# Retention in seven quarter products: keys paired with queries, values with gates

## The chip, the cores and the metric

The kernel runs on one core of a Trainium2 chip. The metric is the device time of one execution in microseconds (us); the time of a kernel is the median of its runs. The engines are named as in the profile: PE (TensorE, matmuls), PEld (its weight loads), DVE (VectorE), ACT (ScalarE), POOL (GpSimd) and SP (SyncE, which here issues the DMAs of the weights).

## The reference

Two layers of a diffusion backbone are computed for 512 latent tokens of width 1024, with 256 context tokens beside them. Layer 0 is windowed attention and a feed-forward; layer 1 is retention and a feed-forward. The change lies in layer 1. With `h_x` and `h_c` the normalised latents and context, cut to what matters:

```python
q_x, k_x, v_x, g_x = split(h_x @ w_qkvg)         # widths 1024, 1024, 2048, 2048
k_c, v_c = split(h_c @ w_qkvg[:, keys and values])
q_x, k_x = rope_2d(q_x), rope_2d(k_x)            # 4 heads: 256 of q and k, 512 of v and g
ox = retention(q_x, k_x, v_x, forward from the context) + the same backward
y = (ox - mean) * rsqrt(var + EPS) * gn_gain      # per head, over its 512
out_x = (silu(g_x) * y) @ w_o
x = x + mx[2] * out_x
x = x + mx[5] * swiglu(modulate(rms_norm(x)), w_in, w_out)
```

All is in float32, and the output is the latent stream.

## The kernel before

Activations lie with channels on the partitions, as eight tiles of 128 channels x 512 tokens for the latents (`xr`, tiles `res`) and 128 x 256 for the context (`cres`). Each float32 operand is split in two float32r parts, `hi` (a copy on ACT) and `lo`, the remainder (a subtraction on DVE); a product is then three matmuls, hi x hi, lo x hi and hi x lo (`mm3`, L145 to L147). `split` (L161 to L163) splits a tile; `next_w` does it for a weight chunk:

```python
def next_w(pool, own=2, raw=None):
    raw = raw or w_raw()
    hi, lo = w_parts(pool, own)
    nc.scalar.copy(hi, raw)                                # L137
    nc.vector.tensor_tensor(lo, raw, hi, op=sub)           # L138
    return hi, lo
```

Weights come as chunks of 128 x 1024 in the order in which they are used, by SP's queue, into two raw buffers (`wraw`); `w_parts` deals out four sets of `whi` and `wlo` in turn. Instructions on an engine run in an order fixed when the kernel is built, by a scheduler that follows the order of the program and the buffers; an instruction waits on its engine, and what is queued behind it waits too. Tiles of one tag take turns in a fixed number of buffers, so a load waits for the last reader of the buffer that it takes.

The retention stage lies at L1074 to L1262, at about 912 to 1454 us of the profiled execution. `norm_mod` (L242; its multiplication L236, its copy and remainder L239 and L240) makes the operand `h[0]` of the latents among the last additions (`gated_add`, L250) of layer 0's feed-forward. Then the loop `for hd in range(RH)` (L1124) goes over the four heads. In each:

- `project` makes queries and keys by channel tile, 96 matmuls of 512 columns each, and the context's keys, 48 of 256. In the first head `context_norm` stands behind the first steps. `rope_pair` (L1094) rotates them, by DVE and POOL (L1101).
- `scores(m)` makes, for six blocks of 128 tokens (four latent, two context), the values (24 matmuls, L1166 to L1168) and the scores (6, L1176 to L1178), and multiplies these by a decay strip (`strips`, L1107, from the table `jt`). `accumulate(m)` (L1189 to L1191) multiplies scores with values into four PSUM halves `ov[n]`, one for each block of query tokens.
- Statistics (L1210), their root on ACT and four scalings (L1220) normalise `ov[n]` to `yn[n]`.
- For each of four channel tiles `e` of the gates: `project` (24 matmuls), silu on ACT (L106), four transposes of `yn` (L1235), a multiplication (L1237), a split of `yt`. PE works on the next tile's projection meanwhile.
- `out_tile(d, c)` (L1243) multiplies by the output weights, 12 matmuls for each of eight channel tiles `d`, and adds to `xr` (L1251).

In the last head `out_tile` goes by halves of 256 tokens, with `add_square` behind each; the first half's norm (`rms`, L210) and its eight `modulate` calls (L232) come behind the second tile of the second half, the second half's norm behind all. The last feed-forward starts with two plain column tiles (`plain`, L1310: X and Y), then token sums (`sums`, L1284) and tiles in seven quarter products (`seven`, L1326; `product`, L826), with 12 matmuls of 256 columns each. Layer 0's feed-forward uses quarter products too.

## Time and profile before

| | |
|---|---|
| median of 3 runs | 1804.34 us (1802.9 to 1807.63) |
| profiled execution | 1810.25 us |
| its span | 1808.5 us |
| granted clock of PE, mean | 0.989 |
| HBM read, written | 174.29 MB, 2.10 MB |
| weight chunks loaded | 214 of 512 KB, median 3.6 us from issue to landing |
| PE on the chain that ended last | 79% of the span |
| DVE, DMA, ACT on that chain | 10%, 3%, 3% |

The span is the time from the first to the last profiled instruction; the profiled execution's time has some overhead around it. A PE matmul's shown duration reaches past the start of the next, so the cost of one in a row of many is the distance of the starts. A row of windows has the limits, the length, then for each engine its busy time and count, the mean granted PE clock (1.00 is full), the DMA share and GB/s. A row of groups has line, engine, operation, tiles out<-in with shapes and count, then total busy us and mean ns of one, then the engine's idle time ahead of them and what ended it. A row of waits has the waiter, the releaser, and total us, times and longest.

### The profile page before, as it was taken

How to read it: one execution, taken by the hardware profiler on the slowest of the kernel's cores; microseconds unless marked ns; L12 is line 12 of the kernel's file. 1: busy time of each engine (PE TensorE's matmuls, PEld its weight loads, DVE VectorE, ACT ScalarE, POOL GpSimd, SP SyncE). 2: the span in 40 equal slices, each digit the busy share in tenths (PEclk: the TensorE clock that was granted, in tenths of full speed). 3: DMA queues.
4: the chain of work that ended last, by engine and by line, in shares of the span. 5: the costliest groups of instructions: out<-in, count | busy, mean ns of one | idle time of the engine just before them, and what ended most of it. 6: DMA issues, size and time to landing. Idle time of an engine off the chain costs nothing.

```text
span 1808.5 us, 26838 instructions
## 1 busy us (share of the span) xinstructions
PE 1754.2 (97%) x10684; PEld 1544.9 (85%) x10684; DVE 1222.8 (68%) x2172; ACT 762.6 (42%) x1340; POOL 152.5 (8%) x283
## 2 busy tenths in 40 slices
PE   6999999999999999999999999999999989999999
PEld 4777777789999999999978888888888889999998
DVE  6697776786688877777693652643543688777774
ACT  5476666454333334342462422322322455445442
POOL 0035334000000000000020010010010000000000
PEclk9999989999999999999999999999999989999999
DMA  8610002434253534443230320320321133234222
GB/s 331 232 36 25 24 1 83 154 114 138 64 156 111 167 124 138 122 140 125 84 95 24 101 85 12 97 79 25 92 70 47 59 105 100 88 117 117 85 91 82
DMA packets 52109, 178.12 MB, mean 98 GB/s; under 512 B 5776, under 2 KB 6160, under 8 KB 51728
## 3 DMA queue, kind: packets, MB, share of 16 engines
q1 hardware_dynamic: 45072, 151.24, 26.1%
q0 software_dynamic: 6912, 25.17, 4.6%
q8 instruction: 84, 1.38, 0.3%
q14 instruction: 41, 0.34, 0.1%
HBM read 174.29 MB, written 2.10 MB: 98 GB/s over the span
## 4 chain that ended last, share of the span: by engine, by line
PE 79%; DVE 10%; DMA 3%; ACT 3%; issue 2%; POOL 2%; SPq 0%; DVEq 0%; POOLq 0%; ACTq 0%
PE Y L826 12%; PE pj L145 8%; PE pj L147 8%; PE pj L146 8%; PE Z L826 6%; PE X L826 3%; PE pv L145 2%; PE pT L698 2%; PE pv L147 2%; PE pv L146 2%; PE pv L1167 2%; PE pv L1168 2%; PE pv L1166 2%; PE S L675 2%; PE pO L710 2%
## 5 line engine op out<-in xcount | busy, mean ns | idle before, releaser
L137 ACT CAST whi<-wraw 128x1024 fp32r<-128x1024 f32 x136 | 142.7, 1050 | 174.8 <-PE pv L147 46.8
L138 DVE TENSOR_TENSOR wlo<-wraw,whi 128x1024 fp32r<-128x1024 f32 x136 | 169.3, 1246 | 52.2 <-ACT whi L137 50.9
L162 ACT CAST whi<-wraw 128x1024 fp32r<-128x1024 f32 x111 | 116.1, 1051 | 186.6 <-PE Z L147 72.6
L826 PE MATMUL Y<-aq,whi 128*128 128x384 f32 x576 | 156.0, 335 | 0.5 <-ACT hn L965 0.5
L163 DVE TENSOR_TENSOR wlo<-wraw,whi 128x1024 fp32r<-128x1024 f32 x111 | 135.2, 1223 | 23.6 <-ACT whi L162 23.2
L145 PE MATMUL pj<-h,whi 128*128 128x512 f32 x320 | 129.2, 404 | 3.5 <-ACT whi L137 3.0
L146 PE MATMUL pj<-h,wlo 128*128 128x512 f32 x320 | 126.3, 395 | 0.8 <-DVE wlo L138 0.8
L147 PE MATMUL pj<-h,whi 128*128 128x512 f32 x320 | 125.9, 395 | 0.0
L250 DVE SCALAR_TENSOR_TENSOR res<-pj,mod,res 128x512 f32<-128x512 f32 (+1 forms) x112 | 81.7, 729 | 64.9 <-PE pj L147 64.0
L826 PEld LDWEIGHTS Y<-aq,whi 128*128 128x128 f32 x576 | 104.8, 188 | 1.4 <-ACT hn L965 0.9
L826 PE MATMUL Y<-aq,wlo 128*128 128x384 f32 x288 | 96.6, 335 | 1.4 <-DVE wlo L163 1.4
L163 DVE TENSOR_TENSOR res<-pv,res 128x512 fp32r<-128x512 f32 x24 | 16.6, 692 | 111.9 <-ACT res L162 111.9
L101 ACT ACTIVATE pr<-pr,stat,qs 128x513 f32<-128x513 f32 (+2 forms) x96 | 74.2, 776 | 32.4 <-DVE stat L682 31.5
L145 PEld LDWEIGHTS pj<-h,whi 128*128 128x128 f32 x320 | 60.8, 190 | 16.8 <-ACT whi L137 5.1
L689 POOL TENSOR_SCALAR pr<-pr,stat 128x512 f32<-128x512 f32 (+2 forms) x96 | 66.9, 710 | 90.8 <-DVE stat L686 66.6
L146 PEld LDWEIGHTS pj<-h,wlo 128*128 128x128 f32 x320 | 60.8, 190 | 12.4 <-DVE wlo L138 1.5
L268 DVE CUSTOM_DVE_ANT_0 y<-adaw,crow,small_sb 128x1024 bf16<-128x1024 f32 x48 | 61.4, 1280 | 14.5 <-DMA adaw<-in_adaT_dram 14.3
L147 PEld LDWEIGHTS pj<-h,whi 128*128 128x128 f32 x320 | 60.6, 189 | 12.0 <-DVE h L240 0.2
L145 PE MATMUL pj<-ax,whi 128*128 128x512 f32 x176 | 68.7, 390 | 0.0
L147 PE MATMUL pj<-ax,whi 128*128 128x512 f32 x176 | 68.6, 390 | 0.0
L146 PE MATMUL pj<-ax,wlo 128*128 128x512 f32 x176 | 68.5, 389 | 0.0
L698 PE MATMUL pT<-const_sb,pr 128*128 128x128 f32 x352 | 58.7, 287 | 9.8 <-POOL pr L689 7.6
(428 smaller groups left out, 5059.5 us busy)
## 6 DMA issues: line engine op xcount, KB each, us to landing
wraw<-in_wst_dram SPq DMA_DIRECT2D x214, 512.0 KB, 3.6
adaw<-in_adaT_dram POOLq DMA_DIRECT2D x32, 512.0 KB, 3.9
adan<-in_adaQ_dram SPq DMA_DIRECT2D x16, 512.0 KB, 7.7
adan<-in_adaN_dram SPq DMA_DIRECT2D x16, 512.0 KB, 8.5
crow<-in_adaT_dram POOLq DMA_DIRECT2D x16, 512.0 KB, 4.2
res<-in_xT_dram SPq DMA_DIRECT2D x16, 256.0 KB, 5.5
adaw<-in_adaT_dram SPq DMA_DIRECT2D x8, 512.0 KB, 3.9
aq<-in_adaN_dram SPq DMA_DIRECT2D x12, 256.0 KB, 6.2
```

The source lines that it names most:

```text
L101: ins = nc.scalar.activation(*args, **kw)
L137: nc.scalar.copy(hi, raw)
L138: nc.vector.tensor_tensor(lo, raw, hi, op=sub)
L145: nc.tensor.matmul(o, whi, xhi, start=first, stop=False)
L146: nc.tensor.matmul(o, wlo, xhi, start=False, stop=False)
L147: return nc.tensor.matmul(o, whi, xlo, start=False, stop=last)
L162: nc.scalar.copy(hi, t)
L163: return nc.vector.tensor_tensor(lo, t, hi, op=sub)
L250: return nc.vector.scalar_tensor_tensor(res[d], o, mods[l, s][:, part, d:d + 1], res[d], mult, add)
L689: nc.gpsimd.tensor_scalar(pt[:, :n], pt[:, :n], st[:, 6 + e:7 + e], 1.0, op0=mult, op1=mult)
L698: nc.tensor.transpose(tp[:, a * P:(a + 1) * P], self.pr[(0, 2, 1, 3)[a]][:, ki * P:(ki + 1) * P], ident)
L826: nc.tensor.matmul(o, p, r, start=first and k + i == 0, stop=k == 3 and i == 2, skip_group_check=not first)
```

## The change

Per head, the latents' keys and queries are now one matrix product of 2 x 2 blocks: two halves of the tokens by two halves of the 1024 channels, times two halves of the channels by (keys, queries). It is done as seven products of blocks instead of eight (Strassen and Winograd's form), with sums of tokens made once for all heads (`token_sums`) and sums of weights made in each head on DVE, in the raw buffers, ahead of the split. Values and gates are a second such product. `product_q` has channels on the partitions of its result and 256 tokens as columns; `product_v` has 128 tokens on the partitions and 512 channels as columns. Values of the latents are thus ready ahead of `scores`; the last two products, for the gates, stand behind `accumulate(5)`. Chunks that serve in a sum and in a product are loaded again, 28 instead of 16 chunks a head, some into a third set of buffers (`wx`). The rope table and the decay table are loaded in each head into one buffer (`rj`). The normalised result stays in PSUM, gates are applied token tile by token tile ahead of the 16 transposes, and the output operand is split out of the transposes' PSUM. In the last head, the weights of the next stage's first two column tiles are split ahead, `modulate` goes tile by tile among the second half's output tiles, and the two first tiles of the feed-forward are computed by halves of tokens (`first_two`), with the second half's norm behind the third step of the first pair. The first weights of the stage are no longer split ahead of its norm. The conditioning columns are computed again where they are needed, and the last feed-forward has its weight sets in a fixed ring of six.

```diff
         bufs = own
-        if wsel[0] % (2 + own) < 2:
+        if ring:
+            pool, bufs = ring[wsel[0] % len(ring)], 2
+        elif wsel[0] % (2 + own) < 2:
             pool, bufs = rp, 2
         wsel[0] += 1
         return T(pool, 1024, "whi", bufs, F32R), T(pool, 1024, "wlo", bufs, F32R)
...
-    wsel[0] = 0
-    wq = [next_w(None), next_w(None)]
+    qw = R.enter_context(tc.tile_pool(name="qw", bufs=1, reuse_waits="tile"))
+    qa = R.enter_context(tc.tile_pool(name="qa", bufs=1, reuse_waits="tile"))
...
+    chunk_base = wpos[0]
+    def chunk(i, own=False):
+        raw = T(qw, 1024, "wx", 4) if own else T(rp, 1024, "wraw", 2)
+        nc.sync.dma_start(raw, wst[i])
+        return raw
+    def split_chunk(raw):
+        w = w_parts(qp)
+        split(raw, *w)
+        return w
+    def operands(first, sums):
+        def of(n):
+            if isinstance(n, int):
+                return lambda k: [a[:, HALVES[n % 2 if n < 3 else n == 3]] for a in sums[2 * k + (n in (2, 3))]]
+            return lambda k: first(4 * (n[1] == "2") + k, int(n[0]) - 1)
+        return of
+    def token_sums(hm, part, sh2, sums):
...
+        for k in range(4):
+            t1, t2 = hm[k], hm[k + 4]
+            nc.vector.scalar_tensor_tensor(t2[:, q2], t1[:, q2], sh2[:, k:k + 1], t2[:, q2], add, add)
+            nc.vector.tensor_tensor(t1[:, q2], t1[:, q1], t1[:, q2], op=sub)
+            nc.vector.scalar_tensor_tensor(t1[:, q1], t2[:, q2], shift[:, k:k + 1], t1[:, q1], sub, sub)
+            nc.vector.scalar_tensor_tensor(t2[:, q1], t2[:, q1], shift[:, k + 4:k + 5], t1[:, q1], add, sub)
+            for i, t in enumerate((t2, t1)):
+                split(t, *sums[2 * k + i])
...
+    quarter_of = operands(first_quarters, h_sum)
...
+    def product_q(o, a, w, first):
+        for k in range(4):
+            xhi, xlo = a(k)
+            for e in range(2):
+                ws = slice(k * 256 + e * P, k * 256 + e * P + P)
+                for i, (p, r) in enumerate(((w[0], xhi), (w[1], xhi), (w[0], xlo))):
+                    ins = nc.tensor.matmul(o[:, e * SC:(e + 1) * SC], p[:, ws], r, start=first and k + e + i == 0,
+                                           stop=k == 3 and i == 2, skip_group_check=True)
+        return ins
+    def product_v(os, a, w, first):
+        for t, o in enumerate(os):
+            tok = slice(t * P, t * P + P)
+            for k in range(4):
+                whi, wlo = (p[:, k % 2 * 512:k % 2 * 512 + 512] for p in w[k // 2])
+                xhi, xlo = (x[:, tok] for x in a(k))
+                for i, (p, r) in enumerate(((xhi, whi), (xhi, wlo), (xlo, whi))):
+                    ins = nc.tensor.matmul(o, p, r, start=first and k + i == 0, stop=k == 3 and i == 2,
+                                           skip_group_check=not first)
+        return ins
...
+        jt = T(qp, 1152, "rj", 1)
+        nc.sync.dma_start(jt, jtab)
...
+    def rope_tables():
+        t = T(qp, 1152, "rj", 1)[:, 0:1024]
+        nc.sync.dma_start(t.rearrange("p (a n) -> p a n", a=2), tabs1)
+        return t[:, 0:512], t[:, 512:1024]
+    hm = latent_norm()
...
+        bq = chunk_base + 16 * hd
+        bv, bg = bq + 4, bq + 8
+        b11 = [split_chunk(chunk(bv + i)) for i in range(2)]
+        b21 = [split_chunk(chunk(bv + i)) for i in (2, 3)]
+        Yv, Xv, cv = [W4("Z"), W4("Z")], [W4("X"), W4("X")], [pj(), pj()]
+        ins = product_v(Yv, quarter_of("11"), b11, True)
         if hd == 0:
+            context_norm([ins])
+        vt = [T(rp, 512, "res", 12) for _ in range(4)]
+        for t in range(2):
+            nc.scalar.copy(vt[t], Yv[t])
+        product_v(Xv, quarter_of("12"), b21, True)
+        for t in range(2):
+            nc.vector.tensor_tensor(vt[t], vt[t], Xv[t], op=add)
+        product_v(cv, context_half(0), b11, True)
+        product_v(cv, context_half(1), b21, False)
+        vt += [T(rp, 512, "y0", 1), T(qp, 512, "vc", 1)]
+        for t in range(2):
+            nc.scalar.copy(vt[4 + t], cv[t])
+        k11, k21 = split_chunk(chunk(bq)), split_chunk(chunk(bq + 1))
+        if hd == 0:
+            token_sums(hm, 0, T(qp, 64, "sh2", 1), h_sum)
+        cos1, sin1 = rope_tables()
+        Y, X, kc = W4("Y"), W4("X"), pj()
+        kt, qt = [[T(qa, 512, "gate", 4) for _ in range(2)] for _ in range(2)]
+        halves = lambda o: enumerate((o[:, 0:SC], o[:, SC:2 * SC]))
+        product_q(Y, quarter_of("11"), k11, True)
+        for e, o in halves(Y):
+            nc.scalar.copy(kt[e][:, HALVES[0]], o)
+        product_q(X, quarter_of("12"), k21, True)
+        for e, o in halves(X):
+            nc.vector.tensor_tensor(kt[e][:, HALVES[0]], kt[e][:, HALVES[0]], o, op=add)
+        product_q(kc, context_half(0), k11, True)
+        product_q(kc, context_half(1), k21, False)
...
+        q12, q22, k11, k21 = chunk(bq + 2, True), chunk(bq + 3, True), chunk(bq), chunk(bq + 1)
+        nc.vector.tensor_tensor(q12, q22, q12, op=sub)
+        nc.vector.tensor_tensor(k11, q12, k11, op=add)
+        w2 = split_chunk(k11)
+        nc.vector.tensor_tensor(k21, k21, k11, op=sub)
+        nc.vector.tensor_tensor(k11, q22, k11, op=sub)
+        w1, w3, w22, w4 = (split_chunk(r) for r in (k11, q12, q22, k21))
+        Y2 = W4("Y")
+        product_q(Y, quarter_of(2), w2, False)
+        for e, o in halves(Y):
+            nc.scalar.copy(qt[e][:, HALVES[0]], o)
+        product_q(Y2, quarter_of(1), w1, True)
+        product_q(Y, quarter_of(3), w3, False)
...
+        product_q(Y2, quarter_of(4), w22, False)
...
+        product_q(Y, quarter_of("22"), w4, False)
...
+        qh = rope_pair(qt, cos1, sin1)
+        kh = rope_pair(kt, cos1, sin1)
+        g12, w2, w4 = [], [], []
+        v11 = []
         for i in range(2):
+            g12.append(chunk(bg + i, True))
+            g22 = chunk(bg + 2 + i)
+            v11.append(chunk(bv + i, True))
+            nc.vector.tensor_tensor(g12[i], g22, g12[i], op=sub)
+            nc.vector.tensor_tensor(v11[i], g12[i], v11[i], op=add)
+            w2.append(split_chunk(v11[i]))
+        w3 = [split_chunk(g) for g in g12]
         for i in range(2):
+            v21 = chunk(bv + 2 + i)
+            nc.vector.tensor_tensor(v21, v21, v11[i], op=sub)
+            w4.append(split_chunk(v21))
+        gate = [T(qa, 512, "gate", 4) for _ in range(4)]
+        product_v(Yv, quarter_of(2), w2, False)
+        for t in range(2):
+            nc.scalar.copy(gate[t], Yv[t])
+        product_v(Yv, quarter_of(3), w3, False)
...
+        product_v(Yv, quarter_of("22"), w4, False)
...
+        ov = [W4("X"), W4("X"), W4("Y"), W4("Y")]
...
+        w1 = []
+        for i in range(2):
+            g, v = chunk(bg + i), chunk(bv + i)
+            nc.vector.tensor_tensor(g, g, v, op=sub)
+            w1.append(split_chunk(g))
+        w22 = [split_chunk(chunk(bg + 2 + i)) for i in range(2)]
+        Zg = [W4("Z"), W4("Z")]
+        product_v(Zg, quarter_of(1), w1, True)
+        for t in range(2):
+            nc.vector.tensor_tensor(gate[2 + t], gate[2 + t], Zg[t], op=add)
+        product_v(Zg, quarter_of(4), w22, False)
+        for t in range(2):
+            nc.vector.tensor_tensor(gate[t], gate[t], Zg[t], op=add)
...
+        for n in (2, 3, 0, 1):
+            silu(gate[n], gate[n])
+            nc.vector.tensor_tensor(gate[n], ov[n], gate[n], op=mult)
+        tps = [W4("Z"), W4("Z"), pj(), pj()]
+        for n in (2, 3, 0, 1):
+            for e in range(4):
+                nc.tensor.transpose(tps[e][:, n * P:(n + 1) * P], gate[n][:, e * P:(e + 1) * P], ident)
         yt = []
         for e in range(4):
...
+            gn = sm_t[:, C_GN + hd * 4 + e:C_GN + hd * 4 + e + 1]
+            hi, lo = t_qk(), t_qk()
+            nc.scalar.activation(hi, tps[e], AF.Identity, scale=gn)
+            nc.vector.scalar_tensor_tensor(lo, tps[e], gn, hi, mult, sub)
             yt.append((hi, lo))
+        wpos[0] = chunk_base + 16 * hd + 12
         w = []
...
+        w += [next_w(qp) for _ in range(4)]
         H.close()
         hF = ctx.enter_context(tc.tile_pool(name="hF", bufs=1, reuse_waits="tile", side="right"))
+        ahead, hx, hm = [], [], []
+        def first_weights(room):
+            raw = w_raw()
+            ahead.append(room())
+            split(raw, *ahead[-1])
+        wx_parts = lambda: (T(qw, 1024, "wx", 4, F32R), T(qw, 1024, "wx", 4, F32R))
+        hF_parts = lambda: (T(hF, 1024, "whi", 2, F32R), T(hF, 1024, "wlo", 2, F32R))
         ln_exp_turn()
         for i, c in enumerate(HALVES):
             for d in range(KT):
-                out_tile(d, c)
-                add_square(0, d, xr[d], c)
+                ins = out_tile(d, c)
+                add_square(0, d, xr[d], c, eng=(nc.vector, nc.gpsimd)[i])
+                if (i, d) in ((0, 5), (0, 7)):
+                    first_weights(wx_parts)
+                if (i, d) in ((1, 3), (1, 5)):
+                    first_weights(hF_parts)
                 if i == 1 and d == 1:
...
                     rms(0, HALVES[0])
-                    for k in range(KT):
-                        modulate(1, 0, 1, k, xr, hx[k], HALVES[0], hm[k][:, HALVES[0]])
-        ahead = [[next_w(None), next_w(None)]]
-        rms(0, HALVES[1])
+                if i == 1 and d > 1:
+                    modulate(1, 0, 1, d - 2, xr, hx[d - 2], HALVES[0], hm[d - 2][:, HALVES[0]], [ins])
+        for k in (KT - 2, KT - 1):
+            modulate(1, 0, 1, k, xr, hx[k], HALVES[0], hm[k][:, HALVES[0]])
+    def second_half(behind):
+        rms(0, HALVES[1], behind=behind)
...
+    ring += [rp, rp, hF, hF, fp, fp]
+    wsel[0] = 4
...
+    def first_two():
+        banks = [(T(psF, 512, "X", 2), T(psF, 512, "Y", 2)) for _ in range(2)]
+        for i, c in enumerate(HALVES):
+            for f, (go, uo) in enumerate(banks):
+                project_pair(ahead[2 * f:2 * f + 2], half(i), (go[:, c], uo[:, c]), None if i + f else second_half)
+        return [finish(*b) for b in banks]
```

249 lines of the change are left out of this document (113 added, 136 removed).

## The prediction

> **What bounds the kernel now.** I read the engine totals first, then the stage that changes in windows, one per head, then the waits of TensorE (PE) in that stage, then single instructions for their durations.
>
> ```profile
> span 1808.5 us, 26838 instructions
> PE 1754.2 (97%) x10684; PEld 1544.9 (85%) x10684; DVE 1222.8 (68%) x2172; ACT 762.6 (42%) x1340; POOL 152.5 (8%) x283
> 996.50:1127.60 131.10, 130.74 (x606) 108.51 (x605) 61.49 (x84) 37.60 (x53) 6.06 (x4) 1.00 0.21 65
> 1127.60:1258.60 131.00, 130.74 (x606) 108.43 (x605) 61.48 (x83) 37.43 (x53) 6.06 (x4) 1.00 0.22 65
> ```
>
> PE is busy 97% of the span. The two windows are the second and third head of the retention (length, then the busy time of PE, its weight loads, VectorE (DVE), ScalarE (ACT) and GpSimd (POOL), then PE's clock). A head takes 131.0 us, PE is busy 130.74 of them at clock 1.00, and DVE has half its time free. So a matmul removed here is worth its spacing, as long as DVE, ACT and the weight loads keep ahead. PE's idle time in the stage sits at its two ends:
>
> ```profile
> PE pv L145 <- DVE res L1251: 5.4, 2, 5.0
> PE X L146 <- DVE wlo L138: 2.8, 1, 2.8
> PE pv L1167 <- DVE wlo L138: 2.1, 2, 1.4
> PE X L145 <- ACT whi L137: 1.3, 1, 1.3
> 945.00:950.00 5.00, 3.65 (x17) 2.73 (x17) 5.00 (x8) 1.94 (x3) 2.88 (x2) 1.00 0.00 0
> ```
>
> The first, second and fourth (5.4, 2.8, 1.3 us in all) stand at the passage to the last feed-forward stage; the third and the window 945 to 950, with DVE at 5.00 of 5, at the start.
>
> **The change part by part.** *1. PE work.* The spacing of matmuls comes from starts, since their shown durations overlap:
>
> ```profile
> 885.97 0.39 PE L146 MATMUL pj<-act,wlo 128*128 128x512 f32 x1
> ...
> 901.84 0.39 PE L147 MATMUL pj<-act,whi 128*128 128x512 f32 x1
> 1515.39 2.83 PE Y L826 x24
> ```
>
> Between the first two rows lie 70 intervals: 15.87/70 = 0.2267 us for 512 columns. The piece of the chain of waits has 24 products of 256 columns: 2.83/24 = 0.118 us, a little over half. Before, a head has 540 matmuls of 512 columns (queries and keys 192, values 144, scores 36, accumulation 72, gates and output 96) and 48 of 256. After, 420 of 512 (seven products of 24 for values and gates, context values 48, scores 36, accumulation 72, output 96) and 216 of 256 (seven products of 24, context keys 48). That is -120 x 0.2267 + 168 x 0.118 = -7.4 us a head, **-29.5** for four. The 16 transposes stay.
>
> *2. The end of a head.* Before, gate tile after gate tile is projected, so PE has 96 matmuls to do while the normalisation runs. After, the last two gate products (48 matmuls, 10.9 us) are the last work; then every gate token tile must be added, passed through silu, multiplied and transposed before the first output tile. The built order of DVE behind the accumulation is: 4 statistics, small operations, 4 scalings, 4 additions and 4 multiplications, and 2 remainders of weights for the output.
>
> ```profile
> L1210 DVE BATCH_NORM_STATS2 bst<-acc 128x6 f32<-128x512 f32 x16 | 10.5, 677 | 0.0
> L1220 DVE TENSOR_SCALAR yn<-acc,mv 128x512 f32<-128x512 f32 x16 | 11.9, 803 | 0.1
> L1251 DVE SCALAR_TENSOR_TENSOR res<-pv,mod,res 128x512 f32<-128x512 f32 x24 | 18.0, 751 | 26.4 <-PE pv L147 26.4
> L138 DVE TENSOR_TENSOR wlo<-wraw,whi 128x1024 fp32r<-128x1024 f32 x70 | 88.4, 1263 | 26.7 <-ACT whi L137 26.1
> L137 ACT CAST whi<-wraw 128x1024 fp32r<-128x1024 f32 x70 | 73.4, 1048 | 96.2 <-PE pv L147 46.8 <-PE pj L147 26.9 <-PE pv L1168 11.9
> L162 ACT CAST yt<-sg 128x512 fp32r<-128x512 f32 x16 | 9.9, 620 | 4.2 <-DVE sg L1237 4.2
> L106 ACT ACT_TABLE_LOAD x5 | 6.4, 1283 | 0.1
> ```
>
> 4 x 0.68 and 1.3 for the small operations (my estimate) make 4.0; 4 x 0.80 + 8 x 0.75 + 2 x 1.26 = 11.7. Consecutive DVE rows overlap by about 0.1 us, so 14.6 us; with the last transposes and the 0.62 us copy of the output operand the first output matmul starts about 16.5 us after the accumulation (silu, its table load of 1.28 and the 1.05 us copies run on ACT beside DVE). PE has 47 matmuls left there (10.65) and about 1.4 us of transposes: idle 4.5 us a head (4 to 6). And an idle PE comes back slow; the nearest rows are the two gaps of the passage:
>
> ```profile
> 1445.00:1450.00 5.00, 0.23 (x1) 0.23 (x2) 5.00 (x14) 2.73 (x6) 0.00 (x0) 0.94 0.00 0
> 1450.00:1455.00 5.00, 5.00 (x32) 4.95 (x32) 3.77 (x9) 1.22 (x4) 0.00 (x0) 0.72 0.38 102
> 1465.00:1470.00 5.00, 2.15 (x14) 1.56 (x13) 5.00 (x14) 3.16 (x5) 0.00 (x0) 0.98 0.02 3
> 1470.00:1475.00 5.00, 3.78 (x17) 3.78 (x18) 5.00 (x9) 3.03 (x6) 0.00 (x0) 0.50 0.54 122
> 1475.00:1480.00 5.00, 5.00 (x38) 5.00 (x38) 4.14 (x6) 3.42 (x5) 0.00 (x0) 0.83 0.57 184
> ```
>
> After 4.77 idle us (1445 to 1450) the clock is 0.72 for 5 us: 1.4 us lost. After 2.85 and 1.22 it is 0.50, then 0.83: 2.5 + 0.85 = 3.35 lost. I take 2.2, nearer to the single gap; a gap that does not cool it costs 0. So 4.5 + 2.2 = 6.7 a head, **+26.8**. The Trainium skill, page "TensorE: Matmul & The Clock Gate", section "Why this matters for your kernels", speaks against this part: keep gaps between matmul bursts under about 3 us, as one idle window brings the clock back to half; the rows agree. By its window of about 3.4 us at half rate (Part 1 of the page) I estimate 1.7 us lost a head, and the part would be +24.8.
>
> *3. Weights in the seven products.* A head now splits 25 chunks instead of 16 and makes 12 sums of whole chunks, but most of this is wanted in the first half of the head, and the sums tie raw buffers together: the first pair of buffers is held until two sums, a remainder, a difference, another and a remainder are done.
>
> ```profile
> wraw<-in_wst_dram SPq DMA_DIRECT2D x214, 512.0 KB, 3.6
> L1101 POOL TENSOR_TENSOR hn<-hn,sq 128x512 f32<-128x512 f32 x16 | 24.2, 1537 | 395.4 <-DVE sq L1100 370.0 <-DVE hn L1099 25.5
> ```
>
> No row shows a sum of weights; the nearest is the remainder, same size, two operands: 1.26. From the key buffers' release to the first gate weights: landing 3.6; five DVE operations and one copy, 7.4; landing 3.6; five operations and two small remainders, 7.1; landing 3.6; sum and remainder 2.5: 27.8 us. PE has in that time six quarter products and the context keys (20 us) and about 4 of the context values: 24.1. The built order puts the first four gate matmuls between query products, so PE waits there, about 3.8 us, with the rest of the query and key products queued behind. A second wait, about 2.2, is on the gate sum's remainder, which stands behind the rope's operations and 1.54 us of POOL each. Both are 6 a head; the first head, with fewer buffers in use, 4: **+22** (0 to 8 a head). The 12 further chunks a head are 12 x 3.6 = 43 us of SP's queue in 131: hidden, as the DMA share of 0.21 leaves room. The reload of rope table and decay table goes through one buffer, `rj`, on SP between chunks: nothing, if strips are computed early.
>
> *4. Start.* Before, the first normalisation runs among the last five additions of the feed-forward's context output:
>
> ```profile
> 910.16 1.24 DVE L236 SCALAR_TENSOR_TENSOR hn<-res,acol,y 128x512 f32<-128x512 f32 x1
> 914.98 0.47 DVE L250 SCALAR_TENSOR_TENSOR res<-Z,mod,res 128x256 f32<-128x256 f32 x1
> L236 DVE SCALAR_TENSOR_TENSOR hm<-res,acol,y 128x256 f32<-128x256 f32 x16 | 7.1, 478 | 0.0
> L163 DVE TENSOR_TENSOR sA<-hm,sA 128x512 fp32r<-128x512 f32 x5 | 3.4, 683 | 0.0
> ```
>
> It starts at 910.16. The built order after has these additions, which wait for PE until about 915, ahead of it, and both remainders of the first weights behind all of it: 8 x 0.75 + 4 x 0.48 + 4 x 0.75 + 1.5 for the strips + 2 x 1.26 = 14.9, so PE starts at 930. Before, it starts at 915 and loses 5 us by 952, so it has done 21.8 us of work at 941.6. After, 10.9 us of products from 930, then the context's products, which wait for the context's normalisation; that and the token sums (16 operations near 0.45, 8 near 0.68) are some 22 us of DVE: 21.8 us of work are done about 955. **+13** (7 if the context comes through first, 18 if the sums do).
>
> *5. Passage to the feed-forward.* Before: 4.77 + 2.85 + 1.22 idle and 1.4 + 3.35 slow clock, 13.6 us. After, the output goes by halves, normalisation among it, weights split ahead, and the second half's sum of squares waits behind the third step of the first pair. One wait is left, for POOL's squares; I take 2 us: **-11.6** (-13.6 to -5).
>
> Costed at nothing: the ring of six weight sets and the other pools in the last stage, and the conditioning columns made again; they issue what was issued before or one small copy under PE's work. If a set came free later, PE would wait for its copy, 1.05 + 1.26 us a time.
>
> Sum: -29.5 + 26.8 + 22 + 13 - 11.6 = +20.7. The profiled execution took 1810.25 us (its span and 1.75 around it), so 1831; it is 5.9 above the median of the three runs, 1804.34, to which the same sum gives **1825**.
>
> **The rivals.** *Covered stalls (faster).* If the remainders come within PE's 24.1 us and the gap of a tail does not cool the clock, part 2 is 4 x 4 and part 3 is 4 x 1: -29.5 + 16 + 4 + 13 - 11.6 = -8.1, 1796. For it: DVE is busy only 61.5 of 131 us. Against: DVE's operations are ordered and the raw buffers make a chain, and DVE's mean says nothing of a chain. It decides at 24.1 us for the first gate weight. *Half the stalls (even).* Parts 2 and 3 at half: -29.5 + 13.4 + 11 + 13 - 11.6 = -3.7, 1801. *Cold at both places (much slower).* If each weight wait also cools the clock, at the upper prices: 4 x 3.35 more there, 4 x 1.15 more at the tails, and part 3 at 8 a head (+10): 20.7 + 28 = 48.7, 1853. For it: waits of 2.85 and 1.22 close together left a clock of 0.50. Against: the waits are split in two by work.
>
> **How the numbers follow.** 0.55 for the forecast, 0.25 for the covered stalls, 0.12 for half, 0.08 for cold at both. A measurement of this kernel tells 0.3%, 5.4 us, from no change: faster 0.25, same 0.12, slower 0.63. Low is the faster rival with part 4 at 7 and the passage at -13.6: 1788. High is the forecast with parts 2 and 3 at their upper bounds (9.35 and 8 a head, +20.6): 1846, and 1848 with a little of part 4.
>
> **What would show it right or wrong.** A head's window should be 131 - 7.4 + 6.7 + 6, about 136 us. At each head's end a gap of 4 to 6 us before the first output matmul, released by the output operand's remainder, and a clock under 0.9 behind it. A wait of the value or gate product for a weight remainder in heads two to four, 3 us or more. PE's first retention matmul at 930. No gap over 3 us at the passage. Heads of 127 us or fewer would make the forecast wrong, and the likely reason is part 3; heads of 142 would be the cold clock.

## The result, and the profile after

The changed kernel takes 1818.82 us (median of five runs, 1813.7 to 1824.14) against 1804.82 of the kernel before (five runs, 1802.9 to 1807.63): ratio 1.0074, 95% interval 1.0049 to 1.0098, 14 us slower. In a second series it took 1814.06 against 1804.34: 1.0050, 1.0037 to 1.0064. The forecast was 1825, slower by 20.7, in a range from 1788 to 1848.

The first lines of its page, spans and engine totals:

```profile
span 1811.9 us, 27643 instructions
PE 1728.4 (95%) x10876; PEld 1531.3 (85%) x10876; DVE 1347.3 (74%) x2327; ACT 836.5 (46%) x1461; POOL 161.6 (9%) x291
```

PE is busy 26 us less and the span is longer. The two traced spans differ by 3.4 us only, and that must not be read as the change's effect: layer 0, which the change leaves alone, ran faster in this execution. The last matmul of layer 0 in the timeline of PE, before and after:

```profile
914.71 0.28 PE L147 MATMUL Z<-act,whi 128*128 128x256 f32 x1
```

```profile
906.14 0.28 PE L149 MATMUL Z<-act,whi 128*128 128x256 f32 x1
```

From there to the end it is 893.8 us before and 905.8 after: +12.0 in the part that changed. The 8.6 us ahead of it go with the clock of those executions (200 to 300 us, for one: 0.93 before, 1.00 after). So I account from the end of layer 0.

The windows from one head's first output matmul to the next head's, for the second to the fourth head:

```profile
1033.68:1170.25 136.57, 128.77 (x652) 107.83 (x652) 89.55 (x118) 55.30 (x81) 7.44 (x4) 0.98 0.37 116
1170.25:1302.93 132.68, 126.02 (x652) 105.90 (x652) 89.46 (x118) 55.46 (x81) 7.43 (x4) 1.00 0.38 119
1302.93:1435.47 132.54, 126.16 (x652) 105.86 (x652) 90.44 (x114) 51.69 (x74) 7.17 (x6) 1.00 0.32 97
```

A head took 131.0 to 131.3 before and takes 132.5 to 136.6 with DVE busy 89 us in place of 61. PE's waits in the stage, from the view of waits:

```profile
PE Z L1179 <- DVE wlo L165: 16.2, 8, 10.2
PE X L147 <- ACT qk L1407: 5.7, 4, 1.6
PE pj L1333 <- DVE hn L1338: 4.1, 3, 1.4
PE Z L1402 <- DVE gate L1396: 3.5, 4, 1.2
PE Z L1179 <- ACT gate L1311: 2.2, 2, 1.9
PE pj L1333 <- ACT qk L164: 2.1, 1, 2.1
PE Y L1167 <- DVE gate L1283: 1.9, 3, 1.0
```

L1179 is a matmul of `product_v`, L1167 of `product_q`, L1333 the first of `scores`, L1402 a transpose of a gated tile, L147 the first output matmul. The first row holds one wait of 10.2, at the start; the second and fourth rows are the heads' tails, four times; the others stand between the query products and the scores, where the gate products lie.

The passage to the last feed-forward, by windows:

```profile
1460.00:1465.00 5.00, 3.64 (x33) 3.45 (x31) 5.00 (x12) 3.98 (x8) 2.37 (x4) 1.00 0.00 0
1465.00:1470.00 5.00, 5.00 (x38) 4.76 (x39) 4.96 (x11) 2.33 (x6) 0.00 (x0) 1.00 0.43 116
1470.00:1475.00 5.00, 5.00 (x45) 5.00 (x44) 4.08 (x11) 3.87 (x7) 0.00 (x0) 1.00 0.31 102
```

One wait of 1.4 to 1.5 us is left (at 1465, for POOL's squares), and the clock stays at 1.00, where it was 0.72, 0.50 and 0.83 in stretches before.

### The profile page after: what moved, and what is told of

Its sections match the earlier page's. It is cut to its first block, busy times and chain, and to the rows that moved or that the text cites. A ratio compares the mean times of both kernels' runs of the same rounds, so it can differ in the third digit from the quotient of the medians.

```text
span 1811.9 us, 27643 instructions
## 1 busy us (share of the span) xinstructions
PE 1728.4 (95%) x10876; PEld 1531.3 (85%) x10876; DVE 1347.3 (74%) x2327; ACT 836.5 (46%) x1461; POOL 161.6 (9%) x291
## 4 chain that ended last, share of the span: by engine, by line
PE 71%; DVE 15%; DMA 5%; ACT 4%; issue 2%; POOL 2%; DVEq 0%; ACTq 0%; POOLq 0%; SPq 0%
PE Y L834 13%; PE Z L834 6%; PE pj L149 6%; PE pj L148 6%; PE pj L147 6%; PE Z L1179 4%; DMA wraw<-in_wst_dram 3%; DVE wlo L165 3%; PE X L834 3%; PE pT L706 2%; PE pO L718 2%; PE S L683 2%; PE pj L1179 2%; PE X L147 1%; PE Y L147 1%
## 5 line engine op out<-in xcount | busy, mean ns | idle before, releaser
L164 ACT CAST whi<-wraw 128x1024 fp32r<-128x1024 f32 x173 | 180.9, 1051 | 307.7 <-PE Z L149 73.1
L165 DVE TENSOR_TENSOR wlo<-wraw,whi 128x1024 fp32r<-128x1024 f32 x173 | 211.1, 1223 | 52.2 <-ACT whi L164 51.7
L139 ACT CAST whi<-wraw 128x1024 fp32r<-128x1024 f32 x84 | 87.9, 1048 | 85.1 <-PE Z L149 23.5
L140 DVE TENSOR_TENSOR wlo<-wraw,whi 128x1024 fp32r<-128x1024 f32 x84 | 102.9, 1226 | 28.1 <-ACT whi L139 27.3
L1179 PE MATMUL Z<-whi,sA 128*128 128x512 f32 x256 | 81.9, 397 | 2.4 <-ACT gate L1311 2.2
L147 PE MATMUL pj<-ax,whi 128*128 128x512 f32 x176 | 68.8, 391 | 1.1 <-DVE res L252 1.1
L1190 POOL TENSOR_TENSOR hn<-hn,sq 128x512 f32<-128x512 f32 x16 | 28.9, 1819 | 448.1 <-DVE sq L1189 432.0
L147 PE MATMUL pj<-act,whi 128*128 128x512 f32 x168 | 66.0, 393 | 0.0
L148 PE MATMUL pj<-act,wlo 128*128 128x512 f32 x168 | 65.9, 392 | 0.0
L149 PE MATMUL pj<-act,whi 128*128 128x512 f32 x168 | 65.5, 390 | 0.0
L706 PEld LDWEIGHTS pT<-const_sb,pr 128*128 128x128 f32 x352 | 38.8, 141 | 30.4 <-POOL pr L697 18.4
L684 DVE CUSTOM_DVE_ANT_0 pr<-S,mask,qs 128x256 f32<-128x256 f32 (+1 forms) x96 | 53.1, 567 | 14.3 <-PE S L683 7.9
```

What stands on the lines that cost most here:

```text
L147: nc.tensor.matmul(o, whi, xhi, start=first, stop=False)
L148: nc.tensor.matmul(o, wlo, xhi, start=False, stop=False)
L149: return nc.tensor.matmul(o, whi, xlo, start=False, stop=last)
L164: nc.scalar.copy(hi, t)
L165: return nc.vector.tensor_tensor(lo, t, hi, op=sub)
L706: nc.tensor.transpose(tp[:, a * P:(a + 1) * P], self.pr[(0, 2, 1, 3)[a]][:, ki * P:(ki + 1) * P], ident)
```

## The experiments

All are compared by the ratio to the kernel before, run in the same series. "Under the changed kernel by the ratios" sets such a ratio against 1.0050, that of the second series of the changed kernel (after_again). Its first series gave 1.0074, so differences of 4 us or less between series are not taken as shown.

**after_again**: the changed kernel once more, unedited.

> The changed kernel once more, beside the kernels of this group. The runs so far spread over 10 us (1813.7 to 1824.1), those of the kernel before over 5. If a cold clock behind the four head tails comes and goes from run to run (theory), the spread is here again, with the mean near 1818. If the spread was an accident of one series (rival), the runs agree within 5 us as those of the kernel before do.

Measured: 1814.06, 1811.61 to 1816.7, ratio 1.0050 (1.0037 to 1.0064). The runs agree within 5 us here, so the spread of 10 was not there again. But the cold clock does move: in the second trace the second head's tail cooled and the fourth's did not; in the first it was the other way round. And in the second trace the third and the fourth head also cooled at a wait for weights (1.7 us each), where the first trace has clock 1.00.

**end_alone**: the passage alone, on the kernel before.

```diff
-                out_tile(d, c)
-                add_square(0, d, xr[d], c)
+                ins = out_tile(d, c)
+                add_square(0, d, xr[d], c, eng=(nc.vector, nc.gpsimd)[i])
                 if i == 1 and d == 1:
                     rms(0, HALVES[0])
-                    for k in range(KT):
-                        modulate(1, 0, 1, k, xr, hx[k], HALVES[0], hm[k][:, HALVES[0]])
-        ahead = [[next_w(None), next_w(None)]]
-        rms(0, HALVES[1])
...
+                if i == 1 and d > 1:
+                    modulate(1, 0, 1, d - 2, xr, hx[d - 2], HALVES[0], hm[d - 2][:, HALVES[0]], [ins])
+                if i == 1 and d in (4, 6):
+                    ahead.append(next_w(None))
...
+                project_pair(ahead[2 * f:2 * f + 2], half(i), (go[:, c], uo[:, c]), None if i + f else second_half)
```

> The kernel before with the passage to the last feed-forward alone changed: modulation tile by tile among the output halves, the second half's norm behind the third step of the first pair, the first two column tiles by halves; only the first pair's weights are split ahead of the passage, as before. Theory (the passage is worth about 10 us and nothing of it depends on the quarter products): 10 us under the kernel before, about 1795; the gaps of 4.8 and 2.9 us are gone. Rival (the idle time only moves into the feed-forward behind it, for the weights of the second pair come too late): a wait of 3 to 6 us at the second pair, and 1800 or more.

Measured: 1796.21 (1795.33 to 1797.31), ratio 0.9953 (0.9940 to 0.9965). The theory held: 8 us, without any quarter product. This version beats both kernels.

**start_first** and **start_lean**: the start.

```diff
+    b11_first = [split_chunk(chunk(chunk_base + 4 + i)) for i in range(2)]
     hm = latent_norm()
...
-        b11 = [split_chunk(chunk(bv + i)) for i in range(2)]
+        b11 = [split_chunk(chunk(bv + i)) for i in range(2)] if hd else b11_first
```

start_lean has, besides, the token sums' operations only for the feed-forward:

```diff
+            if part:
...
```

> The changed kernel with the first head's two value chunks split ahead of the latents' normalisation, so that their remainders stand second and fourth on DVE's order and not behind the whole norm and the strips. Theory (the first product waits for the remainder alone): its wait of 10.4 us shrinks to 1 to 2 us, and the total to 8 us under the changed kernel, about 1810. Rival (DVE is the bound up to the token sums): PE starts earlier and then waits for the context's normalised tiles or the token sums, and the total stays within 2 us of the changed kernel.

> The kernel with the first weights split ahead of the norm, and the 16 arithmetic operations of the retention's token sums left out (their eight splits stay; the output is not the reference's): 16 x 0.42 = 6.7 us less of DVE in the first head alone. Theory (after PE's early start the first head is bound by DVE up to the first scores): the first head up to its first output matmul, 128.1 us there, shrinks by 5 to 7 us, total about 1813 to 1815. Rival (the waits there are for ACT or for weights): under 2 us.

Measured: start_first 1820.32, ratio 1.0082 (1.0068 to 1.0096). The wait of 10 us at the first product is gone, and another stands later, at the first scores. From its view of waits:

```profile
PE pj L1334 <- ACT qk L164: 6.4, 1, 6.4
PE Z L1179 <- DVE wlo L165: 5.9, 6, 1.8
PE X L1179 <- DVE wlo L165: 3.0, 1, 3.0
```

From the end of layer 0 to the first output matmul it is 128.1 us, against 127.5 and 128.7 in the changed kernel's two traces: the rival. Why the whole is 6 us above the changed kernel beside it stays open: from the end of layer 0 to its end the two traces are alike (906.9 and 906.6), and its layer 0, the same program, took 4.8 us longer. start_lean took 1814.11, 1.0051 (1.0031 to 1.0071), and 123.8 us to the first output matmul: 4.3 less for 6.7 us of DVE taken away, a little under what was expected. Of the 4.3, 1.7 are clock (6.8 us were lost in the first head of start_first, 5.1 here), so the waits fell by 2.6. DVE's work is thus a part of the first head's bound and not the whole. The rope is another: in rope_left, below, the first head takes 120.2 us although its start is as late as in the changed kernel, and in all_cut 114.9.

**filler**: 12 matmuls of no use in each tail.

```diff
+        def filler(count, behind):
+            o = W4("Y")
+            s = h_sum[0][0]
+            for i in range(count):
+                ins = nc.tensor.matmul(o, s[:, 0:P], s, start=i == 0, stop=i == count - 1)
+                after(ins, [behind])
...
             for e in range(4):
-                nc.tensor.transpose(tps[e][:, n * P:(n + 1) * P], gate[n][:, e * P:(e + 1) * P], ident)
+                ins = nc.tensor.transpose(tps[e][:, n * P:(n + 1) * P], gate[n][:, e * P:(e + 1) * P], ident)
+            if n < 2:
+                filler(5 + 2 * n, ins)
```

> The changed kernel with 12 matmuls of 512 columns added to each head's tail, 5 between the transposes and 7 behind them, into a free PSUM bank that nothing reads; they take 2.7 us of the 3.1 us that PE idles there. Theory (an idle tail cools the clock in some heads, 2.5 and 1.7 us in the traced run, and more in the slower runs): 4 to 8 us under the changed kernel, 1811 to 1814, with a smaller spread and clock 1.00 behind all four tails. Rival (the clock's loss comes from the transposes, which leave PE as cool as an idle gap): no change, or up to 2 us slower where a filler delays the first output matmul.

Measured: 1813.68, 1.0044 (1.0031 to 1.0056): no change. Windows behind the first tail of the changed kernel, then of filler; and in filler two places where the gate products wait:

```profile
1032.00:1036.00 4.00, 2.79 (x10) 2.06 (x10) 2.91 (x3) 3.72 (x5) 0.00 (x0) 0.54 0.39 122
1036.00:1040.00 4.00, 4.00 (x13) 3.16 (x12) 2.18 (x4) 0.69 (x2) 0.00 (x0) 0.60 0.75 235
```

```profile
1034.00:1038.00 4.00, 3.66 (x17) 2.66 (x16) 2.92 (x3) 3.47 (x6) 0.00 (x0) 1.00 0.35 100
1038.00:1042.00 4.00, 4.00 (x19) 3.29 (x18) 2.92 (x5) 0.68 (x2) 0.00 (x0) 1.00 0.57 211
1252.00:1256.00 4.00, 4.00 (x12) 3.10 (x11) 4.00 (x5) 1.29 (x3) 0.32 (x1) 0.57 0.26 66
1399.00:1403.00 4.00, 4.00 (x11) 3.18 (x11) 3.12 (x4) 1.03 (x2) 0.00 (x0) 0.57 0.33 119
```

All four tails are warm (1.00), as the theory has it, but the second, third and fourth head cool at their weight or score waits, and the clock lost from the end of layer 0 on is 15.4 us in both traces. That the warm tails made the waits cool is not shown: in the second trace of the unedited kernel two heads cool at such waits as well, with 18.8 us lost in all. What the run shows is that warm tails alone do not change the time.

**tail_cut**: the last gate product without its addition.

```diff
-            nc.vector.tensor_tensor(gate[t], gate[t], Zg[t], op=add)
+            nc.vector.tensor_tensor(gate[t], gate[t], gate[t], op=add)
```

> The changed kernel with the last gate product computed but not added (its two additions add the gate to itself, so DVE's work stays). Theory of the forecast (DVE's queue of 15.5 us behind the accumulation sets the first output matmul): the tail's gap stays within 0.5 us of 3.1, the total within 2 us. Rival (the chain behind the last gate product sets it: addition 0.69, silu 0.63, multiplication 0.68, transposes, copy 0.63 and one weight copy of 1.05 on ACT ahead of it): the gap falls to 1 us or less and stays warm, 8 to 13 us under the changed kernel, 1802 to 1806.

Measured: 1806.45, 1.0004 (0.9993 to 1.0014), 8 us under the changed kernel by the ratios. The tail's gap, by the starts of matmuls, is 0.72 in place of 3.1, as the rival has it. But the edit changed two things, and the rows show it. First the third head's tail in the changed kernel (rows of PE, DVE and ACT in order of time, others left out), then the last multiplications and the weight remainders of tail_cut in the same place:

```profile
1285.96 1.29 DVE L1382 BATCH_NORM_STATS2 y<-X 128x6 f32<-128x512 f32 x2
1287.27 0.39 PE L1348 MATMUL Y<-wx 128*128 128x512 f32 x1
...
1297.92 0.40 PE L1179 MATMUL Z<-whi,sA 128*128 128x512 f32 x1
1298.36 0.69 DVE L1371 TENSOR_TENSOR gate<-gate,Z 128x512 f32<-128x512 f32 x1 [0.16 <-PE Z L1179]
1298.96 1.22 DVE L140 TENSOR_TENSOR wlo<-wraw,whi 128x1024 fp32r<-128x1024 f32 x1
1299.08 0.63 ACT L106 ACTIVATE gate<-gate 128x512 f32<-128x512 f32 x1 [1.95 <-DVE gate L1371]
1300.10 0.68 DVE L1396 TENSOR_TENSOR gate<-X,gate 128x512 f32<-128x512 f32 x1
1300.84 0.44 PE L1402 MATMUL Z<-const_sb,gate 128*128 128x128 f32 x2 [1.08 <-DVE gate L1396]
1301.25 1.04 ACT L139 CAST whi<-wraw 128x1024 fp32r<-128x1024 f32 x1 [0.23 <-PE Z L1402]
1302.20 1.26 ACT L1407 ACTIVATE qk<-Z,small_sb 128x512 fp32r<-128x512 f32 x2
1302.93 0.50 PE L147 MATMUL X<-qk,whi 128*128 128x512 f32 x1 [1.44 <-ACT qk L1407]
```

```profile
1295.53 1.28 DVE L1396 TENSOR_TENSOR gate<-X,gate 128x512 f32<-128x512 f32 x2
1296.72 2.35 DVE L140 TENSOR_TENSOR wlo<-wraw,whi 128x1024 fp32r<-128x1024 f32 x2
```

In the changed kernel each step of the chain starts when the one above ends, with two exceptions: the last multiplication (1300.10) stands 0.4 us behind a weight remainder on DVE, and ACT does a weight copy of 1.04 us between the transposes and the output operand. The last addition waited only 0.16 us for the last product (0.12 to 0.16 in the second to fourth head, nothing in the first), as DVE had been busy until then. So DVE's queue and the chain behind the last product are about equally long. In tail_cut the wait for the product is gone, and with it the order changed: both weight remainders now stand behind the multiplications and not among them. The run shows what the two cost together; which of them sets the tail alone stays open.

**no_sums** and **qk_eight**: the weight sums.

```diff
-        nc.vector.tensor_tensor(q12, q22, q12, op=sub)
-        nc.vector.tensor_tensor(k11, q12, k11, op=add)
...
-            nc.vector.tensor_tensor(g, g, v, op=sub)
```

```diff
-        product_q(X, quarter_of("12"), k21, True)
+        product_q(Y, quarter_of("12"), k21, False)
...
+        product_q(X, quarter_of("21"), k11, True)
+        product_q(X, quarter_of("22"), k21, False)
...
+        q12, q22 = (split_chunk(chunk(bq + 2 + i, True)) for i in range(2))
+        for i, o2 in enumerate((Y, X)):
+            product_q(o2, quarter_of("%d1" % (i + 1)), q12, True)
+            product_q(o2, quarter_of("%d2" % (i + 1)), q22, False)
```

> The changed kernel with all 12 weight sums of a head left out (the chunks are split as they come; all loads and splits stay, the output is not the reference's). DVE has 12 x 1.22 = 14.7 us less a head. Theory (sums and the buffers that they hold are what the quarter products wait for): the gaps between head start and accumulation fall from 4.9 us to under 1.5 a head and no clock is lost there: 12 to 18 us under the changed kernel, 1796 to 1802. Rival (those waits belong to the rope's and the scores' operations in DVE's and ACT's order): within 4 us, 1810 or more.

> The changed kernel with keys and queries as eight quarter products in place of seven, without the five weight sums and with two loads less a head; values and gates stay at seven. (The second token half of the first four channel tiles is not kept, and the first half's stands in for it, so the numbers of the output are wrong while the work is that of eight products.) PE has 24 matmuls of 256 columns more a head, 2.83 us, 11.3 in all. Theory (the chain of raw buffers and sums in the query and key part makes the waits of the first gate products, which come with 4.9 us of gaps a head): the gaps fall by 2.5 to 4 us a head, the sum is 0 to -5, 1809 to 1814. Rival (the waits come from DVE's order in the gate and score part): 8 to 11 us slower, 1822 to 1825.

Measured: no_sums 1810.6, 1.0032 (1.0018 to 1.0046), 3 us under the changed kernel by the ratios, with 10 us less of DVE in a head; the third head still takes 133.1 us. qk_eight 1819.1, 1.0074 (1.0056 to 1.0093), 4 us above. Neither difference is clear of that between the two series of the changed kernel. (The edit of qk_eight takes four sums out of a head, not five, and with them three weight splits and six additions.) Their waits for the largest of the kind, no_sums first:

```profile
PE Z L1179 <- DVE wlo L165: 19.0, 9, 10.2
PE X L1339 <- ACT wx L164: 6.6, 4, 2.3
```

```profile
PE pj L1318 <- ACT qk L164: 14.1, 4, 3.5
```

With the sums away, `product_v` waits for weight remainders as before. With four sums and two loads less, the gate products wait no more, and all four heads wait 3.5 us at the scores for ACT's copy of the rotated operand. Neither expectation was met: the first theory fell, the second experiment came out between theory and rival. Both point at the rope.

**rope_dve** and **rope_left**: the rope.

```diff
-            nc.gpsimd.tensor_tensor(a, a, b, op=op)
+            nc.vector.tensor_tensor(a, a, b, op=op)
```

```diff
-            nc.vector.tensor_tensor(b, o[1], f1, op=mult)
-            nc.gpsimd.tensor_tensor(a, a, b, op=op)
```

> The changed kernel with the rope's last operation (four a head, 1.54 us each on POOL) moved to DVE, 0.69 us each; the computation is whole. With the sums left out the waits of the gate products and scores stayed, so the theory is now the rope: its operations go DVE, POOL, ACT, DVE, and the weight remainders and copies queue behind them. Theory (the hop to POOL is what is waited for): the gaps of 4.9 us a head fall by 1 to 2.5, total 3 to 8 us under the changed kernel, 1807 to 1811. Rival (DVE's load is what is waited for; it gets 2.8 us more a head): no change or up to 4 us slower, 1814 to 1819.

> The changed kernel with the rope cut to its first multiplication (four multiplications and all of POOL's operations less a head; the splits stay, the output is not the reference's). Theory (the rope's chain in DVE's and ACT's order makes the waits of gate products and scores): the gaps fall from 4.9 to 1.5 us a head or less, no clock lost there, 10 to 18 us under the changed kernel, 1797 to 1805. Rival (the 25 splits a head make them, with whatever lies between): within 4 us, 1811 or more.

Measured: rope_dve 1809.22, 1.0019 (1.0008 to 1.0029), 5.6 us under the changed kernel by the ratios, as the theory has it, although DVE has 16 operations more. Its busy time in a head hardly rises, 90.4 us against 89.5, since its other operations in the rope are no longer lengthened (last section). rope_left 1794.31, 0.9937 (0.9925 to 0.9949), 20 us under it, more than expected: between head start and accumulation only gaps of 0.4 and 0.9 us are left in the third head. The changed kernel's rope in the third head, from the timelines of DVE, POOL and ACT:

```profile
1243.84 1.76 DVE L1189 TENSOR_TENSOR sq<-gate,rj 128x512 f32<-128x512 f32 x1 [1.19 <-POOL hn L1190]
1245.52 1.21 DVE L165 TENSOR_TENSOR wlo<-wx,whi 128x1024 fp32r<-128x1024 f32 x1
...
1249.67 1.21 DVE L165 TENSOR_TENSOR wlo<-wx,whi 128x1024 fp32r<-128x1024 f32 x1
1252.72 1.11 DVE L165 TENSOR_TENSOR qk<-hn,qk 128x512 fp32r<-128x512 f32 x1 [1.83 <-ACT qk L164]
1253.76 1.22 DVE L165 TENSOR_TENSOR wlo<-wraw,whi 128x1024 fp32r<-128x1024 f32 x1
```

```profile
1249.29 3.99 POOL L1190 TENSOR_TENSOR hn<-hn,sq 128x512 f32<-128x512 f32 x2 [4.24 <-DVE hn L1188]
```

```profile
1252.06 0.62 ACT L164 CAST qk<-hn 128x512 fp32r<-128x512 f32 x1 [3.98 <-POOL hn L1190]
```

POOL waits 4.24 us for a product that stands on DVE behind a weight remainder (1245.52) and three operations of the rope; ACT waits 3.98 for POOL; DVE waits 1.83 for ACT, with the next weight remainder (1253.76) queued behind. The chain goes round through three engines, each in order, and PE's weights sit in between.

**all_cut**: start_lean, rope_left and tail_cut together.

> All cuts together: first weights ahead of the norm, the arithmetic of the token sums and of the rope left out, the last gate additions made independent of their product (the output is not the reference's; PE's work is whole). Theory (PE's saving of 29.5 us and the passage's 8 to 11 are there and only the stalls hide them): the stalls left are some 5 us at the start and 2 a head, so 1770 to 1784. Rival (stalls replace each other, as when one is taken away the next engine is late): 1790 or more.

Measured: 1777.78, 0.9848 (0.9834 to 0.9863). The theory: a second and a third head of 125.6 and 125.4 us, 5.4 and 5.8 under before, with 1.8 to 2.1 us of gaps still in them (the fourth takes 127.5). PE's saving is there; stalls hid it.

**combined**: three repairs with the computation whole: rope_dve, filler, and the two `rope_pair` calls moved.

```diff
-        qh = rope_pair(qt, cos1, sin1)
-        kh = rope_pair(kt, cos1, sin1)
...
         w3 = [split_chunk(g) for g in g12]
+        qh = rope_pair(qt, cos1, sin1)
+        kh = rope_pair(kt, cos1, sin1)
```

> The changed kernel, the computation whole, with three repairs: the rope on DVE without POOL, the rope's operations behind the splits of the gate weights in the program's order, and the 12 filling matmuls of each tail. Theory (waits for the rope and cold tails add up): 5 us for the rope's hop, 3 to 5 for the order, 1 to 3 for the tails: 1800 to 1806, still above the kernel with the passage alone changed (1796). Rival (the rope behind the gate weights makes the scores wait as long as the gate products did): 1808 or more.

Measured: 1795.33 (1792.83 to 1797.51), 0.9947 (0.9929 to 0.9964): better than expected, and 9.6 us under the kernel before. Its heads, by windows:

```profile
1032.88:1162.48 129.60, 128.47 (x666) 107.85 (x664) 91.01 (x123) 56.05 (x82) 0.00 (x0) 1.00 0.38 123
1162.48:1291.94 129.46, 128.18 (x665) 108.05 (x665) 90.17 (x122) 55.24 (x81) 0.00 (x0) 1.00 0.37 123
1291.94:1420.61 128.67, 127.77 (x665) 108.21 (x665) 87.87 (x117) 51.55 (x73) 0.18 (x2) 1.00 0.31 99
```

The clock is 1.00 in these heads, although 2.7 us of each are matmuls of no use. Whether the filling, which brought nothing alone, is needed here was not tested, as no run has the other two repairs without it; in rope_left, whose tails idle while the rope's waits are gone, three of the four tails still cooled, 1.7 us each. The time ties with end_alone, and both contain the passage, so the repaired quarter products have brought nothing beyond it: the second to fourth head take 1.4 to 2.6 us less than before, and the first 9.1 more (123.6 against 114.4).

## Why the prediction was right, and where it was not

The direction and the range were right, and 55% stood on the likeliest case; its size was too large, +20.7 against +14.0 and +9.7 in the two series. By its five terms, from the traces (gaps by the starts of matmuls, lost clock as the sum of 1 minus clock over 1 us windows):

| term | forecast | measured |
|---|---|---|
| PE work | -29.5 | -28.3 |
| tails | +26.8 | +17.6 |
| weights | +22 | +23.8 |
| start | +13 | +8.7 |
| passage | -11.6 | -11.1 |
| sum | +20.7 | +10.7, of +12.0 |

How the rows come out. PE work: in the third heads the median distance of starts is 0.227 us at 512 columns and 0.120, not 0.118, at 256, so -120 x 0.227 + 168 x 0.120 = -7.1 a head and not -7.4. Passage: from the fourth head's first output matmul to the end 376.4 against 385.9, and 1.7 of the 376.4 belong to the cooled tail. Weights: 6.2, 4.9 and 4.8 of gaps in the last three heads, 4.5 of gaps and 3.4 of clock in the first. Start: the first head, from layer 0's end to its first output matmul, is 127.5 against 114.4, +13.1; less 3.6 of tail gap and 7.9 of weights, and 7.1 of PE work added back, 8.7 are left. The last 1.3 us lie in gaps under 0.4 us that no term holds.

*Tails, oversized.* The gap came, at its place, but 2.8 to 3.6 us and not 4.5 (12.5 in all). DVE's queue took what was added up: from the first statistic (1285.96) to the end of the last multiplication (1300.78) it is 14.8 us in the third head, 14.6 in the forecast. But it began 1.5 us before PE was done with the accumulation (1287.50), since the first of its result blocks are complete earlier, and so the first output matmul came 15.4 us behind the accumulation and not 16.5. The forecast also did not price the chain behind the last product, which is about as long as the queue (tail_cut), and the matmul was released by the output operand's copy on ACT, not by its remainder. The clock cooled in two tails of four, for 3.4 and 1.7 us, 5.1 in all, where 8.8 was priced. The rule of the Trainium skill, page "TensorE: Matmul & The Clock Gate", section "Why this matters for your kernels", on gaps over about 3 us agrees in direction only: here gaps of 1.2 to 1.8 us with transposes between cooled the clock in some heads and not in others. My estimate of 1.7 us, from the window of about 3.4 us at half rate in Part 1 of that page, is the loss measured, alone or doubled, at every place in the stage outside its start. The price of 1.4 us that the forecast read behind the gap of 4.77 us was short by the window ahead of it (0.94 for 5 us): it is 1.7 with it, and 3.4 behind the other two gaps.

*Weights, right in size, half wrong in cause.* The first wait of 3.8 us, for the chain of raw buffers, did not come at the first gate matmuls: around them PE waited 0.6 to 1.8 us, in part for DVE to fetch a result (L1283). The second, on a remainder behind the rope and POOL, came as named, with 1.5 to 2.0 in place of 2.2. Two that the forecast did not have stood beside it, at the following product and among the scores (up to 0.7, and 1.6). The first head lost 7.9 us instead of 4. rope_dve and rope_left show that the waits at the products belong to the rope; no_sums shows that they stay when the sums go. The wait among the scores is another matter, and there the chain of raw buffers is at work after all. In the third head:

```profile
1261.18 1.23 DVE L1362 TENSOR_TENSOR wraw<-wraw 128x1024 f32<-128x1024 f32 x1 [3.87 <-DMA wraw<-in_wst_dram]
1263.52 1.22 DVE L165 TENSOR_TENSOR wlo<-wraw,whi 128x1024 fp32r<-128x1024 f32 x1 [1.11 <-ACT whi L164]
1264.66 1.28 DVE L1338 SCALAR_TENSOR_TENSOR hn<-pj,dx 128x512 f32<-128x512 f32 x2
1265.40 0.50 PE L1333 MATMUL pj<-qk 128*128 128x512 f32 x1 [1.37 <-DVE hn L1338]
```

The scores wait for the decay multiplication of an earlier block (L1338). That stands on DVE behind a weight remainder and a weight sum (L1362), and DVE had idled 3.87 us for the sum's raw chunk; in the second and fourth head it was 3.9 and 4.1. That the errors in the single waits nearly cancelled is luck.

*Start, oversized.* The first matmul waited as forecast behind norm and remainders; from the end of layer 0 it came after 13 us, not 15. But start_first shows that undoing this gains nothing, as PE then waits 6.4 us for the rotated operand at the first scores: a term that named the late first matmul named a symptom.

*Passage, right.* One wait, clock warm. end_alone brings 8 of the 11 by itself.

The rival of covered stalls was half right on the clock of the tails. Its point of decision, the first gate weight in time, was nearly met, and yet the products behind it did not run freely: the point was set at the wrong operand. The cold clock at a weight wait, the rival on the slow side, was there in the first head alone; in the changed kernel's second trace it was in the third and fourth as well.

## What to carry to other kernels

When a change trades matmuls for work on other engines, follow one operand round the engines, in each engine's order, before adding up any engine's queue: leaving out half of the rope's multiplications and its POOL operations was worth 20 us, leaving out twelve sums of weights a head 3. Price a stall with the clock behind it, and do not expect to gain by warming one idle place while others are left: filler alone changed nothing. Look whether an edit also changed the order on an engine, as in tail_cut. Split a bundled change: here the passage, which had nothing to do with the rest, was worth 8 us alone and lay hidden under a loss.

## What was not expected of the hardware

In the retention the lost clock comes in two sizes, 1.70 and 3.41 us, in all fourteen traces but at the stage's start (6.83 in nine of them, behind 10 idle us, most of it while PE idles), and the same gap may cost nothing, one or two of them: the second head's tail idled 3.1 us in the first trace of the changed kernel and cost none, 3.0 us in the second and cost 1.70, and in start_first the third head's 3.4 us cost 3.41. Outside the stage 6.83 came once, in layer 0 of the kernel before.

POOL and DVE slow each other in the rope. POOL's operations took 1.82 us on the mean and 1.54 before, and DVE's remainder at 1252.72 took 1.11 where the same shape takes 0.68 elsewhere; it ends 0.55 us after POOL's pair, and the one of 1.76 at 1243.84 ends 0.54 us after the pair before. The Trainium skill, page "SBUF — State Buffer", section "SBUF: two separate sides", says that GpSimd and a DVE operation with two SBUF inputs lock one another out of a shared port pair for a whole instruction; these rows agree. rope_dve bears it out: in the changed kernel 12 of the 56 DVE operations of these three kinds in the four heads (the products that write `sq`, the remainders of the rotated operand and those of the `wx` chunks) are lengthened, to 1.11 to 1.79 from 0.68 and to 2.28 to 2.31 from 1.22, and with POOL's operations gone none is.
